# Attention scores with the queries' lower halves in zero-padded tiles of 128 rows

## The chip, the cores and the metric

The kernel runs on one core of one Trainium2 chip. The metric is device time in microseconds (us), the median over several runs. TensorE (PE in the rows) multiplies, and its weight loads have a row of their own (PEld). VectorE (DVE), ScalarE (ACT) and GpSimd (POOL) work element by element, and SyncE (SP) issues the transfers.

## The reference

Three transformer blocks on 512 tokens of width 1024: feed-forward layers around three kinds of mixer. Three attentions matter here. Each has eight sets of 64-wide queries and keys, and the third block, which has two of the three, runs twice. So there are five attentions in all.

```python
def forgetting_attention(q, k, v, log_f):            # first block
    ...
    for blk in range(s_ // Q_BLOCK):
        q0 = blk * Q_BLOCK
        q1 = q0 + Q_BLOCK
        logits = jnp.einsum('bhqd,bhkd->bhqk', q[:, :, q0:q1], k[:, :, :q1]).astype(jnp.float32) * scale
        ...
        p = jax.nn.softmax(logits, axis=-1).astype(v.dtype)
        outs.append(jnp.einsum('bhqk,bhkd->bhqd', p, v[:, :, :q1]))
...
def diff_mixer(q, k, v, lam, lam_init, g_subln):     # third block, "b"
        ...
        attn = p[:, 0] - lam * p[:, 1]
...
def dsa_mixer(q, k, v, iq, ik, iw):                  # third block, "a"
        ...
        _, idx = lax.top_k(score, topk)
        k_sel = gather(k, idx)
```

Queries stand in blocks of 128, and a block sees the keys up to its own end: 128, 256, 384 or 512 of them.

## The kernel before

The tokens are split in two halves of 256 (`hf` 0 and 1). Each phase (`f10`, `m1`, `f11`, ..., `m30`, `f30`, `m31`, `f31`) is written for half 0 and then for half 1, and priorities with a lag between the halves let a list scheduler weave them into one fixed order per engine when the program is built. While one half is in a mixer's attention, the other half's large products fill TensorE. The engines then run their orders strictly in sequence. `m1` is the first block's mixer, `m30` and `m31` are the third block's mixer in its two layers.

Numbers are held as two fp16 halves, upper and lower. For large products, `three` forms three matmuls of 128 rows by 256 columns: upper by upper, upper by lower, lower by upper. A head of the attention has only 64 rows, so the halves are stacked. `Heads` keeps a key's upper half on 64 rows and its lower half on the other 64 (tile `hd`). For queries the upper half stands twice in `hd`, and the lower half stands once, on the head's own 64 rows, in `hl`. In `scores`, one matmul over 128 rows then gives upper query times both halves of the key, and a second one over 64 rows adds lower query times upper key:

```python
mm(s[:, c0:c0 + n], q.t[j // 2][:, j % 2, e, c], k[:, :n], start=c0 == 0, stop=False)
mm(s[:, c0:c0 + n], q.low[r, j, c], k[r, :n], start=False, stop=False)
```

`e` is 0 or 1, and says which 64 rows are the head's. `keys(nk)` cuts the keys into pieces of at most 256, one for each half's tile. The 128 or 256 keys of a piece are the columns that the matmul streams. After the scores come a mask product, `softmax` (a maximum on VectorE, an exponential on ScalarE), `transposed` (TensorE, with a copy on ScalarE) and the product with the values.

In a printed form such as `64*128 64x256` the first number is the rows of the array that a matmul uses, and the last the columns streamed.

Query tiles come from the pool `mid` (`m2k`), which has 11 buffers for each half. The feed-forward layers' `act` tiles, the rotation tables, the indexer's scores and the attention's outputs come from the same pool. A buffer is given out again once its last tile has been read.

Of the kernel before, what the change touches and what calls it, by code (L numbers as in the profile page):

```python
# [11 lines left out]
F16 = mybir.dt.float16  # L12
# [7 lines left out]
TH = 256  # L20
# [36 lines left out]
# ---------------------------------------------------------------- host layout  # L57
# [99 lines left out]
def prepare(inp):  # L157
    a = {}
# [4 lines left out]
    # first block  # L163
# [21 lines left out]
    # second block  # L185
# [18 lines left out]
    # third block  # L204
# [36 lines left out]
# ---------------------------------------------------------------- the kernel  # L241

@with_exitstack
def tile_three_blocks(ctx: ExitStack, tc: tile.TileContext, d, col_at, con_at, out, phases=None):
# [42 lines left out]
    # ---- allocation  # L287
# [25 lines left out]
    def mm(out_, l, r, start=True, stop=True):  # L313
        return PE.matmul(out_, lhsT=l, rhs=r, start=start, stop=stop, skip_group_check=True)  # L314

    # ---- constants
# [33 lines left out]
    # ---- weights  # L350
# [45 lines left out]
    # ---- small functions  # L396
# [145 lines left out]
    # ---- conditioning of the first block  # L542
# [50 lines left out]
    # ---- token-major products  # L593
# [21 lines left out]
    # ---- softmax attention  # L615
# [20 lines left out]
    class Heads:  # L636
        """Eight heads of 64 rows, each as the fp16 halves of its values: stacked for keys, and for queries the
        upper half twice, with the lower half by itself."""

        def __init__(self, alloc, hf, query):  # L640
            self.t = [alloc(hf, [128, 2, 2, TH], F16, "hd") for _ in range(2)]
            self.low = alloc(hf, [128, 4, TH], F16, "hl") if query else None

        def put(self, j, src, scale=None):
            t = self.t[j // 2][:, j % 2]
            for e in range(2):
                a, b = slice(64 * e, 64 * e + 64), slice(64 - 64 * e, 128 - 64 * e)
                hi = t[a, e]
                lo = t[b, e] if self.low is None else self.low[a, j]
                if scale is None:  # L650
                    S.activation(hi, src[a], AF.Copy)
                    V.tensor_tensor(lo, src[a], hi, op=OP.subtract)
                else:
                    S.activation(hi, src[a], AF.Copy, scale=scale)
                    V.scalar_tensor_tensor(lo, src[a], scale, hi, op0=OP.mult, op1=OP.subtract)  # L655
                if self.low is not None:
                    S.activation(t[b, e], hi, AF.Copy)

    def scores(s, q, ks, j, e, c, nk):
        r = slice(64 * e, 64 * e + 64)  # L660
        for kh, c0, n in keys(nk):
            k = ks[kh].t[j // 2][:, j % 2, e]
            mm(s[:, c0:c0 + n], q.t[j // 2][:, j % 2, e, c], k[:, :n], start=c0 == 0, stop=False)
            mm(s[:, c0:c0 + n], q.low[r, j, c], k[r, :n], start=False, stop=False)
# [15 lines left out]
    # ---- the first block's mixer  # L680
# [3 lines left out]
    def mixer1(hf):  # L684
# [22 lines left out]
        # keys and queries  # L707
# [8 lines left out]
        # forget gates  # L716
# [26 lines left out]
        # values  # L743
# [5 lines left out]
        # attention  # L749
# [23 lines left out]
        # gated unit: projections  # L773
# [33 lines left out]
        # gated unit: spatial product  # L807
# [44 lines left out]
    # ---- the second block's mixer  # L852
# [3 lines left out]
    def mixer2(hf):  # L856
# [32 lines left out]
        # projections with token shift  # L889
# [23 lines left out]
        # convolution branch  # L913
# [32 lines left out]
        with boost(BOOST["m2k"]):  # L946
            wau = kv2k(0, name="wau")
            nc.sync.dma_start(out=wau, in_=d["m2_wa"])
            S.activation(xwa[0:64], xwa[0:64], AF.Tanh)
            S.activation(xg, xg, AF.Tanh, scale=0.5)  # L950
            V.tensor_scalar(xg, xg, 0.5, 0.5, op0=OP.mult, op1=OP.add)
            # key norms
            pn = psmall(hf, [8, TH], name="pkn")
            for q in range(4):
                t = t1k(hf, name="ksq")
                S.activation(t, kk_(q), AF.Square, scale=col("k_k", q))
                mm(pn, m2["sel8"][:, q * 8:q * 8 + 8], t, start=q == 0, stop=q == 3)
            kn = t1k(hf, [8, TH], name="kn")
            V.tensor_scalar(kn, pn, 1e-12, None, op0=OP.max)
            kr = t1k(hf, [8, TH], name="kr")  # L960
            rsqrt(hf, kn, kr)
            zb = {}
            wc = tin.tile([128, 4, 4], F32, name="wc", tag=f"wc{hf}", bufs=1)
            c64 = lambda ap: ap.rearrange("p (c t) -> p c t", c=2)

        def prep(pc):
            for q in range(4):
# [4 lines left out]
                # decay  # L972
# [12 lines left out]
                # write rate  # L985
# [4 lines left out]
                # normalised keys  # L990
# [20 lines left out]
        # values by token  # L1011
# [12 lines left out]
        # recurrence, by chunks  # L1024
# [63 lines left out]
        def chunk(c):  # L1088
# [5 lines left out]
            # products of queries and keys  # L1094
# [13 lines left out]
            # state in, corrections, outputs  # L1108
# [52 lines left out]
        with boost(BOOST["m2c"]):  # L1161
            mix = mixed[0]
            # gate
# [7 lines left out]
            # group norm and output  # L1171
# [49 lines left out]
    # ---- the third block's mixer  # L1221
# [3 lines left out]
    def mixer3(hf, l):  # L1225
# [37 lines left out]
        # projections of the indexer  # L1263
# [23 lines left out]
        # scores and selection  # L1287
# [41 lines left out]
        # projections and the difference of attentions  # L1329
# [15 lines left out]
        with boost(BOOST["m3b"]):  # L1345
            for qt in range(2):
                nk = (2 * hf + qt + 1) * 128
                nb = nk // 128
                # difference of attentions
# [21 lines left out]
        # projections of the selected attention  # L1371
# [15 lines left out]
        with boost(BOOST["m3a"]):  # L1387
            for qt in range(2):
                nk = (2 * hf + qt + 1) * 128
                nb = nk // 128  # L1390
                # selected attention
# [17 lines left out]
    # ---- the end  # L1409
# [10 lines left out]
    # ---- the order of the phases  # L1420
# [60 lines left out]
# ---------------------------------------------------------------- launch  # L1481
# [17 lines left out]
```

## Time and profile before

| | |
|---|---|
| median of 3 runs | 3520.48 us (3518.86 to 3536.04) |
| span of the profiled execution | 3506.1 us, from its first instruction to its last |
| PE busy | 3321.3 us (95%) |
| PEld busy | 2794.6 us (80%) |
| DVE busy | 2173.5 us (62%) |
| ACT busy | 1541.9 us (44%) |
| POOL busy | 0.2 us (four small memsets) |
| mean granted TensorE clock | 0.989 of full speed |

The profile gives the span alone of its execution; the median of the runs is 14.4 us above that span, which is what lies around it. Busy shares are means over stages that have different limits, so a stage is read for itself.

### The profile page before, as it was taken

To read this page: it belongs to the slowest core of one execution; us is meant where nothing else is said; L and a number is where in the kernel's file an instruction comes from. 1 tells how busy PE (TensorE), PEld (TensorE's weight loads), DVE (VectorE), ACT (ScalarE), POOL (GpSimd) and SP (SyncE) were. 2 spreads that over 40 slices of the span, in tenths; PEclk is the share of its full clock that TensorE was granted. 3 is DMA by queue.
4 is the path that set the end of the run, shared out by engine and by line. 5 is a ranking of instruction groups with operands and counts; after the bars stand their busy time and mean duration, and the time that the engine had idled before them with its cause. 6 is when DMAs were issued, how large, how long until landed. Compare 5 with 4: busy or idle time off the path is not lost.

```text
span 3506.1 us, 71906 instructions
## 1 busy us (share of the span) xinstructions
PE 3321.3 (95%) x30158; PEld 2794.6 (80%) x30164; DVE 2173.5 (62%) x5240; ACT 1541.9 (44%) x3335; POOL 0.2 (0%) x4
## 2 busy tenths in 40 slices
PE   5999999999999999997799998899999998999998
PEld 4888866788888888886578887667888876678887
DVE  8953757844374437588874438886544488855433
ACT  3332466433243324424243336886333378743331
POOL 0000000000000000000000000000000000000000
PEclk9999999999999999998899999999999999999999
DMA  8932313133223232201023232112232321023321
GB/s 275 324 112 91 118 55 130 61 103 103 97 92 103 98 102 91 76 5 35 31 74 106 100 105 79 55 49 67 91 103 104 100 78 61 31 79 109 102 98 48
DMA packets 105590, 327.88 MB, mean 94 GB/s; under 512 B 12584, under 2 KB 18088, under 8 KB 105008
## 3 DMA queue, kind: packets, MB, share of 16 engines
q1 hardware_dynamic: 105264, 323.28, 27.4%
q8 instruction: 236, 3.87, 0.4%
q14 instruction: 90, 0.74, 0.1%
HBM read 321.14 MB, written 2.10 MB: 92 GB/s over the span
## 4 chain that ended last, share of the span: by engine, by line
PE 75%; DVE 12%; ACT 9%; DMA 2%; issue 2%; SPq 0%; DVEq 0%; ACTq 0%
PE pgu L314 37%; PE po L314 19%; PE ps L314 5%; PE pp L314 4%; ACT rsw L1258 2%; PE pt L314 2%; DVE wr L363 2%; DVE mix L939 1%; ACT wr L362 1%; DMA st<-in_gu_dram 1%; PE pgl L314 1%; PE pxy L314 1%; DVE acc L433 1%; PE ps L631 1%; PE pT L314 1%
## 5 line engine op out<-in xcount | busy, mean ns | idle before, releaser
L314 PEld LDWEIGHTS <-wr 128*128 128x128 f16 x24000 | 2346.4, 98 | 322.7 <-issue 22.4
L314 PE MATMUL pgu<-hh,wr 128*128 128x256 f16 x12672 | 1400.1, 273 | 8.2 <-ACT wr L362 2.3
L363 DVE SCALAR_TENSOR_TENSOR wr<-st,wr 128x1024 f16<-128x1024 f32 x524 | 640.0, 1222 | 350.6 <-ACT wr L362 341.8
L314 PE MATMUL po<-act,wr 128*128 128x256 f16 x6336 | 700.3, 273 | 0.1
L362 ACT ACTIVATE wr<-st 128x1024 f16<-128x1024 f32 x524 | 551.5, 1053 | 322.5 <-PE pgu L314 127.6
L314 PE MATMUL pp<-hh,wr 128*128 128x256 f16 x3072 | 376.5, 273 | 4.0 <-DVE hd L655 1.2
L523 ACT ACTIVATE fth<-pgu 128x256 f32<-128x256 f32 x264 | 101.0, 383 | 587.2 <-PE pgu L314 587.1
L524 DVE SCALAR_TENSOR_TENSOR fth<-fth,pgu 128x256 f32<-128x256 f32 x264 | 110.8, 420 | 356.8 <-ACT fth L523 356.8
L314 PE MATMUL po<-mix,wr 128*128 128x256 f16 x1536 | 198.0, 281 | 15.8 <-ACT mix L444 9.0
L444 ACT ACTIVATE act<-fac 128x256 f16<-128x256 f32 x264 | 109.8, 416 | 179.1 <-DVE fac L526 179.1
L314 PE MATMUL pt<-wr,hh 128*128 128x512 f16 x576 | 146.2, 383 | 2.0 <-DVE wr L363 1.8
L445 DVE TENSOR_TENSOR act<-fac,act 128x256 f16<-128x256 f32 x264 | 111.2, 421 | 50.6 <-ACT act L444 50.2
L492 DVE TENSOR_TENSOR acc<-acc,sq 128x256 f32<-128x256 f32 x84 | 35.3, 420 | 149.6 <-ACT sq L491 149.6
L1258 ACT ACTIVATE rsw<-pp 32x256 f32<-32x256 f32 x304 | 114.1, 375 | 18.1 <-PE pp L314 13.6
L526 DVE SCALAR_TENSOR_TENSOR fac<-fth,pgu 128x256 f32<-128x256 f32 x264 | 110.7, 419 | 7.7
L619 DVE TENSOR_REDUCE amx<-ps 128x1 f32<-128x128 f32 (+3 forms) x160 | 77.8, 488 | 60.4 <-PE ps L314 55.7
L485 ACT ACTIVATE y<-po 128x256 f32<-128x256 f32 x64 | 24.4, 382 | 204.6 <-PE po L314 204.6
L432 ACT ACTIVATE sq<-x 128x256 f32<-128x256 f32 x154 | 56.3, 409 | 131.8 <-DVE x L501 127.4
L939 DVE SCALAR_TENSOR_TENSOR mix<-glu,cols,mix 128x256 f32<-128x256 f32 x240 | 101.9, 474 | 0.1
L314 PEld LDWEIGHTS <-hh 128*128 128x128 f16 x768 | 62.3, 100 | 48.0 <-issue 4.7
L565 DVE SCALAR_TENSOR_TENSOR ada<-adw,csil,ada 128x512 f32<-128x512 f32 x126 | 90.9, 744 | 7.2 <-DMA adw<-in_w_ada_dram 7.0
L501 DVE SCALAR_TENSOR_TENSOR x<-po,x 128x256 f32<-128x256 f32 x64 | 26.8, 421 | 106.8 <-PE po L314 106.8
(355 smaller groups left out, 2889.4 us busy)
## 6 DMA issues: line engine op xcount, KB each, us to landing
st<-in_gu_dram SPq DMA_DIRECT2D x264, 512.0 KB, 3.5
st<-in_dn_dram SPq DMA_DIRECT2D x132, 512.0 KB, 3.5
adw<-in_w_ada_dram SPq DMA_DIRECT2D x144, 256.0 KB, 5.5
st<-in_m_o_dram SPq DMA_DIRECT2D x32, 512.0 KB, 3.5
st<-in_m_b_dram SPq DMA_DIRECT2D x16, 512.0 KB, 3.5
st<-in_m_a_dram SPq DMA_DIRECT2D x16, 512.0 KB, 3.5
st<-in_m_s_dram SPq DMA_DIRECT2D x14, 512.0 KB, 3.5
st<-in_m_qk_dram SPq DMA_DIRECT2D x8, 512.0 KB, 4.4
```

The lines of the kernel that those rows point to most:

```text
L314: return PE.matmul(out_, lhsT=l, rhs=r, start=start, stop=stop, skip_group_check=True)
L362: S.activation(r[:, 0], st, AF.Copy, scale=WS)
L363: V.scalar_tensor_tensor(r[:, 1], st, WS, r[:, 0], op0=OP.mult, op1=OP.subtract)
L444: S.activation(hi, src, AF.Copy)
L445: V.tensor_tensor(lo, src, hi, op=OP.subtract)
L523: S.activation(t, p[:, 0], AF.Tanh, scale=0.5 / WS)
L524: V.scalar_tensor_tensor(t, t, 1.0, p[:, 0], op0=OP.add, op1=OP.mult)
L526: V.scalar_tensor_tensor(a, t, 0.5 / WS / WS / AS, p[:, 1], op0=OP.mult, op1=OP.mult)
L565: V.scalar_tensor_tensor(ada_acc[g, h], src, csil[:, k:k + 1], ada_acc[g, h], op0=OP.mult, op1=OP.add)
L619: V.tensor_reduce(nm, s[:, :nk], axis=AX.X, op=OP.max, negate=True)
L939: V.scalar_tensor_tensor(cc(j), gl[:, i:i + TH], dw[:, j * 31 + i:j * 31 + i + 1], cc(j), op0=OP.mult, op1=OP.add)
L1258: S.activation(sw[a:a + 32], p[c:c + 32], AF.Copy, scale=scale)
```

## The change

There are now two lower tiles per set of queries, one for each `e`. Each has 128 rows: the head's 64 rows carry the lower half, and the other 64 are set to zero on GpSimd when the tiles are made. The second score product then runs over all 128 rows, with the whole key tile as the moving side; the zero rows add nothing to the sum. The diff also replaces comments by blank lines, which moves line numbers by two to four.

```diff
         def __init__(self, alloc, hf, query):
             self.t = [alloc(hf, [128, 2, 2, TH], F16, "hd") for _ in range(2)]
-            self.low = alloc(hf, [128, 4, TH], F16, "hl") if query else None
+            self.low = [alloc(hf, [128, 4, TH], F16, "hl") for _ in range(2)] if query else None
+            if query:
+                for e in range(2):
+                    G.memset(self.low[e][64 - 64 * e:128 - 64 * e], 0.0)
...
-                lo = t[b, e] if self.low is None else self.low[a, j]
+                lo = t[b, e] if self.low is None else self.low[e][a, j]
...
     def scores(s, q, ks, j, e, c, nk):
-        r = slice(64 * e, 64 * e + 64)
         for kh, c0, n in keys(nk):
             k = ks[kh].t[j // 2][:, j % 2, e]
             mm(s[:, c0:c0 + n], q.t[j // 2][:, j % 2, e, c], k[:, :n], start=c0 == 0, stop=False)
-            mm(s[:, c0:c0 + n], q.low[r, j, c], k[r, :n], start=False, stop=False)
+            mm(s[:, c0:c0 + n], q.low[e][:, j, c], k[:, :n], start=False, stop=False)
```

The order of instructions on TensorE, VectorE and ScalarE is the same as before in all phases but `m30` and the stretch of `f30` that is woven with it. GpSimd has new work. Its order before, from the start of the program to its end:

```order
L1488 MEMSET const-float32-0.0 128x1
L1488 MEMSET const-float32-1.0 128x1
L1488 MEMSET const-bfloat16-1.0 128x1
L1488 MEMSET const-uint8-127 128x1
L1494 UNCONDITIONAL_BRANCH x2
```

And now, from the branch into the program on, with what each instruction waits for (semaphores of engines and of transfers; the first four `hl` are `m1`'s, the next two are `m30`'s half 0, "b", the next two half 0, "a", the last two shown half 1, "b"):

```order
L1496 UNCONDITIONAL_BRANCH [waits barrier_Pool_Activation_PE_DVE_SP_gather]
L645 MEMSET hl_4933 64x1024 [waits DVE_49,PE_49]
L645 MEMSET hl_4934 64x1024 [waits DVE_49,PE_49]
L645 MEMSET hl_6468 64x1024 [waits DVE_49,PE_49]
L645 MEMSET hl_6469 64x1024 [waits DVE_49,PE_49]
L645 MEMSET hl_26209 64x1024 [waits DVE_49,PE_49,Pool_49]
L645 MEMSET hl_26210 64x1024 [waits DVE_49,PE_49]
L645 MEMSET hl_26931 64x1024 [waits DMAHW2_49,DVE_49]
L645 MEMSET hl_26932 64x1024 [waits DMAHW1_49,DVE_49]
L645 MEMSET hl_28414 64x1024 [waits DMAHW7_49,PE_49,Activation_49]
L645 MEMSET hl_28415 64x1024 [waits PE_49,Activation_49,Pool_49]
```

Twenty memsets of 64 rows by 1024 elements are new, two for each of the ten sets of queries; each waits for the last users of the buffer that it takes.

The second place is TensorE in `m30`, where half 0's first score pass of "b" begins. Before (`pd` is the indexer's product, `ps` a score, `pp` a projection):

```order
L314 LDWEIGHTS iq
L314 MATMUL pd<-ik,iq 128x256
L314 LDWEIGHTS hd
L314 MATMUL ps<-hd 128x128
L314 LDWEIGHTS hl
L314 MATMUL ps<-hd,hl 128x128
L314 LDWEIGHTS identb
L314 MATMUL ps<-maskb,identb 128x128
L314 LDWEIGHTS wr
```

Now:

```order
L314 MATMUL pp<-hh,wr 128x256
L314 LDWEIGHTS iq
L314 MATMUL pd<-ik,iq 128x256
L314 LDWEIGHTS iq
L314 MATMUL pd<-ik,iq 128x256
L314 LDWEIGHTS hd
L314 MATMUL ps<-hd 128x128
L314 LDWEIGHTS hl
L314 MATMUL ps<-hd,hl 128x128
L314 LDWEIGHTS identb
L314 MATMUL ps<-maskb,identb 128x128
```

The same three products of a score stand together, but five projection matmuls have moved ahead of the two indexer products and the score. No order shows the rows of the array; the `hl` product has 64 before and 128 now.

The third place is VectorE in `m30`, where the two halves write their lower query tiles. Before (`hl_28402` is half 1's "b", `hl_26922` is half 0's "a"):

```order
L652 TENSOR_TENSOR hl_28402<-rot_28595,hd_28400 64x256
L1261 TENSOR_TENSOR rot_27095<-rot_27095,rsw_27126 128x256
L626 RECIPROCAL ars_26877<-asm_26875 128x1
L1311 MEMSET sc_28166 64x64
L363 SCALAR_TENSOR_TENSOR wr_27144<-st_27142,wr_27144 128x1024
L652 TENSOR_TENSOR hl_28402<-rot_28595,hd_28400 64x256
L1259 SCALAR_TENSOR_TENSOR rot_28635<-pp_28636,rope64_27993 128x256
L1260 TENSOR_TENSOR rsw_28661<-rsw_28661,rope64_27993 128x256
L652 TENSOR_TENSOR hl_26922<-rot_27095,hd_26920 64x256
```

Now (`hl_26932` is one of half 0's "a" tiles, `hl_28414` one of half 1's "b"):

```order
L405 TENSOR_SCALAR drs_26910<-drs_26910 128x4
L1261 SCALAR_TENSOR_TENSOR rot_28650<-pp_28651,rope64_28005 128x256
L1262 TENSOR_TENSOR rsw_28676<-rsw_28676,rope64_28005 128x256
L626 RECIPROCAL ars_27387<-asm_27385 128x1
L407 SCALAR_TENSOR_TENSOR rsa_26911<-drs_26910,dss_26780 128x4
L1263 TENSOR_TENSOR rot_28650<-rot_28650,rsw_28676 128x256
L408 TENSOR_TENSOR rsa_26911<-rsa_26911,drs_26910 128x4
L655 TENSOR_TENSOR hl_26932<-rot_27152,hd_26929 64x256
L409 SCALAR_TENSOR_TENSOR drs_26910<-rsa_26911,drs_26910 128x4
L1316 MAX m8_28250<-sc_28178 128x8
L407 SCALAR_TENSOR_TENSOR rsa_26911<-drs_26910,dss_26780 128x4
L655 TENSOR_TENSOR hl_28414<-rot_28570,hd_28412 64x256
```

Before, half 1's "b" query tiles came first and half 0's "a" after them; now half 0's "a" is written ahead of the first of half 1's "b".

## Rows read from the trace of the kernel before

**Rows 1.** The page: its span, and the busy time of TensorE and the others.

```profile
span 3506.1 us, 71906 instructions
PE 3321.3 (95%) x30158; PEld 2794.6 (80%) x30164; DVE 2173.5 (62%) x5240; ACT 1541.9 (44%) x3335; POOL 0.2 (0%) x4
```

**Rows 2.** Timeline, PE: start us, us, instruction, xcount, idle time before it.

```profile
3087.55 0.27 PE L314 MATMUL ps<-hd 128*128 128x256 f16 x1
3087.76 0.28 PE L314 MATMUL ps<-hd,hl 64*128 64x256 f16 x1
3087.97 0.28 PE L314 MATMUL ps<-hd 128*128 128x256 f16 x1
3088.18 0.28 PE L314 MATMUL ps<-hd,hl 64*128 64x256 f16 x1
3088.39 0.39 PE L314 MATMUL ps<-mb,identb 128*128 128x512 bf16 x1
...
460.29 0.22 PE L314 MATMUL ps<-hd 128*128 128x128 f16 x1
460.44 0.23 PE L314 MATMUL ps<-hd,hl 64*128 64x128 f16 x1
460.60 0.23 PE L314 MATMUL ps<-cum,sel 72*128 72x128 bf16 x1
```

**Rows 3.** Timeline, PE and PEld, where products without a 64-row one follow one another.

```profile
499.60 7.59 PE L314 MATMUL pp<-hh,wr 128*128 128x256 f16 x68
...
499.71 7.30 PEld L314 LDWEIGHTS <-wr 128*128 128x128 f16 x67
...
457.66 0.22 PE L314 MATMUL ps<-maskb,identb 128*128 128x128 bf16 x1
457.72 0.22 PE L314 MATMUL ps<-cum,sel 72*128 72x128 bf16 x1
```

**Rows 4.** Windows: us, busy of each engine, granted clock, DMA share, GB/s.

```profile
415.00:600.00 185.00, 179.74 (x1302) 123.06 (x1303) 128.01 (x375) 113.48 (x282) 0.00 (x0) 1.00 0.27 89
2150.00:2340.00 190.00, 167.33 (x1292) 117.54 (x1289) 168.96 (x492) 161.48 (x425) 0.00 (x0) 0.99 0.13 43
2340.00:2480.00 140.00, 138.13 (x1058) 104.05 (x1062) 92.04 (x238) 84.12 (x228) 0.00 (x0) 1.00 0.19 61
2840.00:3020.00 180.00, 157.13 (x1197) 108.86 (x1196) 157.19 (x461) 149.02 (x397) 0.00 (x0) 1.00 0.14 47
3020.00:3120.00 100.00, 98.57 (x716) 70.16 (x717) 66.23 (x167) 69.58 (x191) 0.00 (x0) 1.00 0.19 64
```

**Rows 5.** The same windows, instructions with `hl` alone: PE, PEld, DVE.

```profile
415.00:600.00 185.00, 12.57 (x48) 4.44 (x48) 6.73 (x16) 1.00 0.27 89
2150.00:2340.00 190.00, 11.34 (x44) 4.07 (x44) 9.95 (x24) 0.99 0.13 43
2340.00:2480.00 140.00, 13.79 (x52) 4.81 (x52) 3.32 (x8) 1.00 0.19 61
2840.00:3020.00 180.00, 12.81 (x50) 4.62 (x50) 9.97 (x24) 1.00 0.14 47
3020.00:3120.00 100.00, 12.33 (x46) 4.26 (x46) 3.31 (x8) 1.00 0.19 64
```

**Rows 6.** Chain that ended last, by line, shares of windows 2150:2340 and 2840:3020.

```profile
by line: ACT rsw L1258 19.6%; PE pp L314 10.4%; PE pt L314 8.6%; PE ps L314 8.0%; ACT hd L651 5.8%; issue 4.6%; ACT prob L624 4.6%; ACT wr L362 4.3%; ACT hd L657 3.9%; ACT rl L1305 2.5%; DVE hd L652 2.2%; ACT probt L633 2.2%; ACT ps L1364 1
...
by line: ACT rsw L1258 21.2%; PE ps L314 12.4%; PE pp L314 9.8%; PE pt L314 8.8%; ACT hd L651 8.2%; ACT prob L624 5.3%; ACT hd L657 4.8%; issue 4.2%; ACT wr L362 3.9%; ACT rl L1305 3.0%; ACT probt L633 2.5%; ACT hh L444 1.6%; ACT ps L1364 1
```

**Rows 7.** Those two windows, instructions with `ps` alone: PE, PEld, DVE, ACT.

```profile
2150.00:2340.00 190.00, 39.45 (x206) 10.71 (x88) 14.12 (x31) 32.20 (x114) 0.99 0.13 43
2840.00:3020.00 180.00, 45.65 (x245) 13.60 (x109) 15.07 (x35) 36.90 (x132) 1.00 0.14 47
```

**Rows 8.** Groups by line, memsets on VectorE and GpSimd: busy us, mean ns | idle.

```profile
L871 DVE MEMSET state<- 128x512 f32 x1 | 0.5, 485 | 0.1
...
L1488 POOL MEMSET const-uint8-127<- 128x1 uint8 x1 | 0.1, 102 | 0.0
```

## The prediction

> **What bounds the kernel now.** I read the page first: the span is 3506.1 us and TensorE is busy for 95% of it [rows 1]. With nothing else, that says only that TensorE matters. So the next view is the windows around the attentions [rows 4]. There the reader is to see two sorts of stretch. In 415 to 600 (`m1`), 2340 to 2480 (the end of `m30`) and 3020 to 3120 (the end of `m31`) TensorE is busy for 97 to 99%, and VectorE and ScalarE for 60 to 70%: what TensorE no longer does there is taken off the end. In 2150 to 2340 and 2840 to 3020 (the first parts of `m30` and `m31`) TensorE is at 87 to 88%, VectorE at 87 to 89%, ScalarE at 83 to 85%: three engines wait for one another in turn, and the chain there runs over ScalarE's rotation copies (20 and 21%) before any line of TensorE's [rows 6]. The same windows with `hl` alone count the second score products: 48, 44, 52, 50 and 46, 240 in all [rows 5].
>
> Then the timeline of single score products, where start to start counts and the printed lengths don't (they hold the latency of the array, which overlaps). Within a score of 512 keys the four products of 256 columns start at 3087.55, .76, .97 and 3088.18, and the mask product at 3088.39: 0.21 us each [rows 2]. Where every product uses all rows, 68 of the same 256 columns take 7.59 us, of which 0.27 is the last one's length: 7.32 / 67 = 0.109 us each, and their 67 weight loads lie beside them [rows 3]. So a product on 64 rows costs about 0.10 us more to go into and about 0.10 us more to leave. For 128 columns the steps are 0.15 and 0.16 us [rows 2], against 0.06 where two of 128 columns follow each other without a 64-row one [rows 3].
>
> **What the change removes.** A second product over 128 rows is the same kind of instruction as the first. Per product of 256 columns: from 0.84 us for two pairs to four times 0.109 = 0.436, so 0.40 / 2 = 0.20 us. Per product of 128 columns: 0.31 less two steps of 0.06, so 0.19 us. By the loops, each of five attentions with eight heads has per head two pieces of 128 columns (at 128 and 384 keys) and four of 256: 80 and 160 in all, which makes the 240 counted. Sum of TensorE's time: 160 x 0.20 + 80 x 0.19 = 47.2 us, 0.197 us on the mean.
>
> How much of it reaches the end is taken by stretch. In the three full ones lie 48 + 52 + 46 = 146 products: 146 x 0.197 = 28.8 us, taken whole. In the two mixed ones lie 94: 18.5 us, between nothing (ScalarE and VectorE set the pace, and TensorE only waits longer) and all of it. I choose by how much of the score work there lies on the chain: the line `ps` of the matmul helper has 8.0% of 190 us and 12.4% of 180 us, 15.2 + 22.3 = 37.5 us [rows 6], of 39.45 + 45.65 = 85.1 us of `ps` work on TensorE [rows 7]. That is 44%, so 8.1 us. Together 36.9 us.
>
> One rule speaks against this term. The rows show weight loads lying beside full-array products: 67 loads in 7.30 us under 68 matmuls in 7.59 [rows 3]. The Trainium skill (TensorE: Matmul & The Clock Gate, Part 3: Packing small matmuls) says that weight loads overlap with matmuls in flight only when they go to other row groups. By that rule a full second product would wait for its load behind the first, and padding would gain nothing; the rows of the full-array products don't bear it out, since there every load goes to all rows.
>
> **What it adds.** Twenty memsets of 64 x 1024 on GpSimd, which does nothing else. The trace has none of this size. VectorE's 128 x 512 memset takes 485 ns, GpSimd's 128 x 1 takes 102 ns [rows 8]. From below I take 0.1 us each, from above four times VectorE's rate, 4 x 2 x 0.485 = 3.9 us; it is nearest in kind to VectorE's, so 1 us, as an estimate. I put none of it on the path. The cover: a set's key projections stand ahead of its query projections, four of 24 matmuls, 96 x 0.109 = 10.5 us of TensorE, and the memset is issued where the set is made. Were that cover gone, the first score product of each tile would wait, 20 x 1 = 20 us, and the gain would be 17.
>
> VectorE writes as many elements to `hl` as before, in the same instructions. The weight load of an `hl` tile takes 92 ns on the mean (4.44 us for 48 [rows 5]), a full one at most 109 (67 in 7.30 us [rows 3]), and it lies beside the product before it. It costs nothing while products take 0.109; where products have 128 columns the load is the longer, and 0.06 to 0.07 a step is what the rows show.
>
> **What it moves.** One more buffer of `mid` is held for each set of queries. In `m1` and `m31` the orders are unchanged, so nothing moves. In `m30` half 0's first score falls behind five projection products on TensorE (0.5 us), and half 0's "a" tiles come ahead of half 1's "b" on VectorE; behind these stand the maxima and the selection, for which ScalarE's exponentials and then TensorE's transposes wait. Its price can't be read from an order. TensorE idles for 190 - 167.3 = 22.7 us in the first part of `m30` [rows 4]; a worse weave could add a third to it, a better one take a third away: -7 to +7 us. I take 0, since the same work stands in both orders and the end of `m30` is full of TensorE's work.
>
> **The sum.** 3506.1 - 36.9 = 3469.2 us of span. The profiled execution has no time of its own beside its span; the median of the runs is 14.4 us above it, and I carry that over: 3520.5 - 36.9 = 3483.6, 3484 us, 1.0% less.
>
> **The rivals.**
> All of it arrives: the mixed stretches are chains of products, softmax steps and copies, and a score that ends sooner lets its maximum start sooner. For it: in those windows TensorE waits in turn with the others, not for one alone. Against it: ScalarE's rotation copies lead the chain there. 3520.5 - 47.2 = 3473 us.
>
> Only the full stretches pay and `m30`'s new weave costs 7 us: 28.8 - 7 = 21.8, so 3499 us. Against it: half 0's scores move by half a microsecond only.
>
> The change doesn't do what it says: the second product waits for its own weight load even over full rows. Then a step costs 0.109 for the product and 0.09 to 0.11 for the load, 0.20 to 0.22 us, what it costs now, and the time stays at 3520 us. Against it stand the 67 loads beside full products.
>
> Slower: the zeros are late. In `m3` the memsets wait for buffers that VectorE, ScalarE and transfers must free, and they stand in one queue on GpSimd; TensorE stands in order, and the first weight load of each `hl` tile waits for GpSimd with all of the other half's products queued behind it. There are 16 such tiles in `m30` and `m31`. It makes the kernel slower than before from 36.9 / 16 = 2.3 us a tile on; with 5 us each, 80 - 36.9 = 43 us, 3564 us. Against it: the 10.5 us of key products ahead, and idle GpSimd.
>
> **How the numbers follow.** The forecast has 0.65, all of it 0.14, the full stretches alone with a bad weave 0.11, no effect 0.05, late zeros 0.05. The measurement can tell about 0.5%, 17.6 us, from no change, so faster means under 3503. Of the bad weave's 0.11 I count 0.07 as faster and 0.04 as the same (it may cost some more than 7). That gives faster 0.86, same 0.09, slower 0.05. The likeliest time is 3484; the range reaches from 3468 (all of it, with 5 us from a better weave) to 3503 (the full stretches alone, less 11 us for weave and memsets), which leaves out no effect, late zeros and a part of the bad weave.
>
> **What would show it.** In the profile after: score products in a row start 0.11 us apart with 256 columns and 0.06 to 0.07 with 128; the printed shape is `128*128` for all 480. `m1` from its first to its last score is shorter by about 48 x 0.197 = 9.5 us. The first parts of `m30` and `m31` are shorter by 3 to 5 us each, and TensorE's busy share there falls. GpSimd's memsets end before VectorE writes the same tile's query halves, and no weight load of `hl` waits for GpSimd. The prediction is wrong if the steps stay at 0.2 us, if `m30` gets longer while `m31` gets shorter (weave), or if waits of TensorE for `hl` and GpSimd appear.

## The result, and the profile after

The changed kernel takes 3507.4 us (median of 5 runs, 3493.8 to 3521.6), the kernel before 3523.4 us (5 runs beside them). The ratio is 0.9939 with an interval of 0.991 to 0.9968: about 0.6% faster. In two later sets of runs the ratio was 0.9967 (0.995 to 0.9985) and 0.9933 (0.9908 to 0.9958). So the gain is 0.3 to 0.7%, 12 to 24 us, where 36.9 us and 1.0% were forecast. 3507 lies 4 us above the range's upper end; by the ratio and the 3520.5 us from which the sum was made it is 3499.

The page of the changed kernel, its span and busy times, against [rows 1]:

```profile
span 3506.0 us, 71986 instructions
PE 3309.1 (94%) x30164; PEld 2815.7 (80%) x30164; DVE 2171.3 (62%) x5240; ACT 1545.5 (44%) x3335; POOL 19.1 (1%) x24
```

By these two pages nothing was won: 3506.0 us now, 3506.1 before. They are single executions, and the reader should not stop here; where they differ is shown below.

The timeline of TensorE in the changed kernel, at the score of 512 keys that [rows 2] shows:

```profile
3087.66 0.27 PE L314 MATMUL ps<-hd 128*128 128x256 f16 x1
3087.77 0.27 PE L314 MATMUL ps<-hd,hl 128*128 128x256 f16 x1
3087.88 0.27 PE L314 MATMUL ps<-hd 128*128 128x256 f16 x1
3087.99 0.27 PE L314 MATMUL ps<-hd,hl 128*128 128x256 f16 x1
3088.10 0.38 PE L314 MATMUL ps<-mb,identb 128*128 128x512 bf16 x1
```

The steps are 0.11 us where they were 0.21, and the shape is `128*128`. Four products take 0.44 us in place of 0.84. With 128 columns the steps are 0.06 us, as the rows of 2958.49 and 2958.55 below show.

The windows of the changed kernel. Their edges lie at the same instructions as those of [rows 4], so the lengths can be compared; only the edges at 2350.5 and 2488.5, where the order has moved, are the nearest that fit (columns: window; us; busy of PE, PEld, DVE, ACT, POOL; granted clock; DMA share; GB/s):

```profile
414.50:593.50 179.00, 173.17 (x1303) 123.78 (x1304) 127.69 (x375) 113.69 (x282) 0.00 (x0) 1.00 0.28 91
2160.50:2350.50 190.00, 164.01 (x1289) 120.85 (x1286) 168.44 (x496) 158.33 (x421) 4.73 (x5) 0.96 0.13 43
2350.50:2488.50 138.00, 131.53 (x1063) 104.46 (x1061) 92.22 (x235) 88.65 (x233) 0.00 (x0) 1.00 0.19 62
2848.40:3024.40 176.00, 149.85 (x1197) 110.54 (x1195) 156.26 (x461) 149.27 (x397) 1.89 (x2) 0.99 0.16 49
3024.40:3119.10 94.70, 91.77 (x717) 70.69 (x717) 65.64 (x168) 69.48 (x191) 0.00 (x0) 1.00 0.22 68
```

Against [rows 4] the five windows are shorter by 6.0, 0.0, 2.0, 4.0 and 5.3 us. That is 17.3 us of 36.9. The two windows of `m30` give 2.0, where 3.8 + 10.2 = 14.0 were forecast (44 x 0.197 x 44%, and 52 x 0.197). The granted clock of the first of them is 0.96, where it was 0.99; more on that below.

GpSimd's memsets, as a group of the changed kernel (busy us, mean ns | idle before them, by releaser):

```profile
L645 POOL MEMSET hl<- 64x1024 f16 x20 | 18.9, 946 | 2938.2 <-PE po L314 2249.0 <-DVE acc L492 371.8 <-DVE rsw L1262 109.6
```

One takes 0.946 us; 1 us was the estimate. In each of the three profiles of the changed kernel a single wait of TensorE or its weight loads is put down to GpSimd, in `m31`, and it is 1.0 us long. The rows around it, in this profile:

```profile
2956.59 0.94 POOL L645 MEMSET hl<- 64x1024 f16 x1 [74.97 <-DVE rsa L407]
...
2958.28 0.27 PE L314 MATMUL ps<-hd 128*128 128x256 f16 x1 [0.72 <-ACT rl L1307]
2958.28 0.10 PEld L314 LDWEIGHTS <-hl 128*128 128x128 f16 x1 [1.00 <-POOL hl L645]
...
2958.49 0.22 PE L314 MATMUL ps<-hd 128*128 128x128 f16 x1
...
2958.55 0.22 PE L314 MATMUL ps<-hd,hl 128*128 128x128 f16 x1
```

The memset had ended at 2957.54, 0.74 us before the load began. The load began together with the product ahead of it, and that one had waited for ScalarE's `rl`. So the memset isn't what held TensorE there.

**Why two equal spans hide a gain.** The rows of a tile give the starts of its first and of its last instruction, and so the ends of a phase. Three lengths were taken, all from start to start: `m1` from its first to its last score product (`ps<-hd`), from the first rotation copy (`rsw<-pp`) of `m30` to that of `m31` (`m30` with `f30`), and from there to the last score product of `m31`. The rows of the kernel before, by tile (count: shortest/median/longest ns, first to last start; shapes):

```profile
L314 PE MATMUL ps<-hd x48: 216/269/283, 431.2 to 575.5; 128*128 128x256 f16 x32, 128*128 128x128 f16 x16
...
L1258 ACT ACTIVATE rsw<-pp x152: 373/375/380, 2143.4 to 2364.6; 32x256 f32<-32x256 f32 x152
...
L1258 ACT ACTIVATE rsw<-pp x152: 373/375/378, 2800.0 to 3043.8; 32x256 f32<-32x256 f32 x152
...
L314 PE MATMUL ps<-hd x96: 216/269/283, 2850.5 to 3101.8; 128*128 128x256 f16 x64, 128*128 128x128 f16 x32
```

Of the changed kernel:

```profile
L314 PE MATMUL ps<-hd x48: 216/269/283, 430.7 to 568.8; 128*128 128x256 f16 x32, 128*128 128x128 f16 x16
...
L1260 ACT ACTIVATE rsw<-pp x152: 373/376/378, 2153.8 to 2376.5; 32x256 f32<-32x256 f32 x152
...
L1260 ACT ACTIVATE rsw<-pp x152: 373/376/382, 2808.4 to 3047.0; 32x256 f32<-32x256 f32 x152
...
L314 PE MATMUL ps<-hd x96: 216/269/417, 2858.9 to 3101.0; 128*128 128x256 f16 x64, 128*128 128x128 f16 x32
```

`m1` took 575.5 - 431.2 = 144.3 and takes 138.1 us; `m30` with `f30` took 656.6 and takes 654.6; `m31` took 301.8 and takes 292.6. The three together are 17.4 us shorter. But from `m1`'s last score product to `m30` it took 1567.9 us before and takes 1585.0, 17.1 more, and no score product lies there. The windows of 1340 to 1800 us, in the second block's mixer `m2`, show what differs; first the kernel before in its first profile, then the changed kernel, then the kernel before profiled again:

```profile
1340.00:1800.00 460.00, 405.90 (x4830) 334.99 (x4828) 380.58 (x1144) 191.31 (x440) 0.00 (x0) 0.93 0.15 50
```

```profile
1340.00:1800.00 460.00, 406.33 (x4690) 333.99 (x4688) 366.66 (x1097) 184.94 (x425) 0.00 (x0) 0.89 0.15 47
```

```profile
1340.00:1800.00 460.00, 410.11 (x4660) 336.17 (x4657) 362.15 (x1088) 182.19 (x418) 0.00 (x0) 0.87 0.15 46
```

The granted clock is 0.93, 0.89 and 0.87, and the same 460 us hold 4830, 4690 and 4660 matmuls. The kernel before thus has both the quick and the slow version of this stretch: profiled again, it reaches `m30` 2163.3 - 2143.4 = 19.9 us later, while its three lengths are 144.3, 656.6 and 301.7 us, the same to 0.1. What `m2` does to a span differs from execution to execution and is as large as the effect looked for; the three lengths of the kernel before are not touched by it. They are the measure in what follows, beside the timed ratios. They aren't free of the clock either: the changed kernel's `m30` with `f30` took 654.6, 653.1 and 651.9 us in three executions of the same order, with 13.7, 10.2 and 6.8 us of it at the lower clock level, 1.2 GHz.

### The profile page after: what moved, and what is told of

Its sections match the earlier page's. It is cut to its first block, busy times and chain, and to the rows that moved or that the text cites. A ratio compares the mean times of both kernels' runs of the same rounds, so it can differ in the third digit from the quotient of the medians.

```text
span 3506.0 us, 71986 instructions
## 1 busy us (share of the span) xinstructions
PE 3309.1 (94%) x30164; PEld 2815.7 (80%) x30164; DVE 2171.3 (62%) x5240; ACT 1545.5 (44%) x3335; POOL 19.1 (1%) x24
## 5 line engine op out<-in xcount | busy, mean ns | idle before, releaser
L314 PEld LDWEIGHTS <-wr 128*128 128x128 f16 x24000 | 2351.0, 99 | 327.8 <-issue 25.5
L314 PE MATMUL pgu<-hh,wr 128*128 128x256 f16 x12672 | 1402.6, 273 | 7.9 <-ACT wr L362 2.3
L314 PE MATMUL po<-act,wr 128*128 128x256 f16 x6336 | 702.0, 273 | 0.1
L314 PE MATMUL pp<-hh,wr 128*128 128x256 f16 x3072 | 384.1, 274 | 4.8 <-DVE rot L1261 2.2
L314 PE MATMUL po<-mix,wr 128*128 128x256 f16 x1536 | 198.0, 282 | 15.9 <-ACT mix L444 9.0
L314 PE MATMUL pt<-wr,hh 128*128 128x512 f16 x576 | 145.4, 383 | 1.6 <-DVE wr L363 1.6
L314 PEld LDWEIGHTS <-hh 128*128 128x128 f16 x768 | 62.2, 100 | 48.3 <-issue 3.2
```

## The experiments

Twelve runs were made, of seven further kernels and of the two that are compared. What was timed (median of all runs in us; ratio to the kernel before on the same chip, with its interval) and the three lengths, as differences from 144.3, 656.6 and 301.8 us:

| kernel | timed | ratio | `m1` | `m30` + `f30` | `m31` | together |
|---|---|---|---|---|---|---|
| changed kernel | 3507.4 | 0.9939 (0.991 to 0.9968) | -6.2 | -2.0 | -9.2 | -17.4 |
| e0_after | 3512.9 | 0.9967 (0.995 to 0.9985) | -6.5 | -4.7 | -9.5 | -20.7 |
| a_again | 3499.7 | 0.9933 (0.9908 to 0.9958) | -5.0 | -3.5 | -10.1 | -18.6 |
| e1_full_one_tile | 3494.5 | 0.9916 (0.9893 to 0.9939) | -6.5 | -7.9 | -9.7 | -24.1 |
| e1_again | 3493.4 | 0.9919 (0.9892 to 0.9945) | -6.5 | -8.3 | -9.6 | -24.4 |
| e2_two_tiles_64 | 3524.7 | 1.0006 (0.9987 to 1.0026) | 0.0 | +4.9 | -0.2 | +4.7 |
| e2_again | 3513.2, one run | | 0.0 | +4.8 | +0.5 | +5.3 |
| h2_no_memset_64 | 3521.3, one run | | 0.0 | -1.2 | +1.2 | 0.0 |
| e3_grouped | 3508.0 | 0.9958 (0.9937 to 0.9979) | -3.1 | -4.5 | -3.8 | -11.4 |
| f1_pool_copy | 3489.8 | 0.9904 (0.9878 to 0.993) | -7.1 | -8.5 | -14.9 | -30.5 |
| b_again (the kernel before) | 3528.0, one run | | 0.0 | 0.0 | -0.1 | -0.1 |
| d0_double_copy | 3533.7, one run | | +1.5 | +5.7 | +14.2 | +21.4 |
| d1_double_copy_full | 3522.2, one run | | -5.2 | +0.7 | +6.5 | +2.0 |

The theory was that a change between 64-row and 128-row products costs time on either side of a 64-row one, and that a part of what is shed is lost to `m30`'s new weave and to waits in the full stretches. The rivals were that the second tile and the zeros cost the difference directly, and that the 64-row product itself is slow.

**The full second product without second tiles** (e1_full_one_tile). The kernel before, with one line changed. The one lower tile holds the other head's lower half on the other 64 rows, so each score gets one term more, that half by this key's lower half.

```diff
-            mm(s[:, c0:c0 + n], q.low[r, j, c], k[r, :n], start=False, stop=False)
+            mm(s[:, c0:c0 + n], q.low[:, j, c], k[:, :n], start=False, stop=False)
```

> The kernel before with one edit: the second score product runs over all 128 rows of the single lower tile and of the key tile. No zeros, no memset, no second tile. The rows of the other head are not zero, so the scores also get the other head's lower query half times this key's lower half, which the kernel before leaves out. My theory (the steps of the products fall from 0.2 to 0.11 us, about 0.12 us of each 0.197 reaches the end in full stretches, and the extra tiles' new weave in m30 costs some us): about 25 to 32 us faster than before, 3 to 8 us better than the changed kernel. Rival one, the new weave costs nothing: the same as the changed kernel within 3 us. Rival two, the second product is slow for its zero rows or its two tiles: no faster than the changed kernel, whatever the order.

Ratio 0.9916, 27.6 us by the medians, where 25 to 32 were expected. Against the changed kernel it is better by 18.4 us in this set of runs (e0_after) and by 6.4 in the next, where 3 to 8 were expected; the repeats below bear on that. In `m1` and `m31` it gains what the changed kernel does, in `m30` 7.9 us in place of 2.0 to 4.7. Its rotation rows give that length, 2798.3 - 2149.6 = 648.7 us:

```profile
L1258 ACT ACTIVATE rsw<-pp x152: 372/374/380, 2149.6 to 2366.9; 32x256 f32<-32x256 f32 x152
...
L1258 ACT ACTIVATE rsw<-pp x152: 372/374/378, 2798.3 to 3036.4; 32x256 f32<-32x256 f32 x152
```

So the product over all rows is the gain, and what comes with the two tiles takes some of it back in `m30`. This kernel's order isn't wholly that of before: VectorE and ScalarE keep it in `m1` and in `m30` up to 2366 us of the first trace, and some fifty instructions of each are moved behind that, most of them at the end of `m30`.

**The two tiles without the full product** (e2_two_tiles_64). The tiles, the memsets and the order of the changed kernel, with the second product on 64 rows:

```diff
-            mm(s[:, c0:c0 + n], q.low[e][:, j, c], k[:, :n], start=False, stop=False)
+            r = slice(64 * e, 64 * e + 64)
+            mm(s[:, c0:c0 + n], q.low[e][r, j, c], k[r, :n], start=False, stop=False)
```

> The changed kernel with the second score product put back to 64 rows: the two lower tiles, the twenty memsets and the new order in m30 stay. My theory: 0 to 7 us slower than before, all of it in m30; m1 and m31 as before within 1 us. Rival (tiles, memsets and weave are free): the same as before within 2 us in every mixer. Second rival (late zeros): waits of TensorE's weight loads of the lower tiles for GpSimd, 2 us or more each.

Ratio 1.0006. `m1` and `m31` stay within 0.2 us; `m30` becomes 4.9 us longer:

```profile
L1261 ACT ACTIVATE rsw<-pp x152: 372/374/377, 2154.1 to 2379.7; 32x256 f32<-32x256 f32 x152
...
L1261 ACT ACTIVATE rsw<-pp x152: 372/374/378, 2815.6 to 3059.3; 32x256 f32<-32x256 f32 x152
```

661.5 us against 656.6. The padding's companions cost about 5 us, all in the one phase whose order moved; 0 to 7 were expected. The effects add up: -24.1 + 4.7 = -19.4, and the changed kernel has -17.4 to -20.7.

**The 64-row products side by side** (e3_grouped). The kernel before, with a score's upper products first and its 64-row ones behind them:

```diff
-        for kh, c0, n in keys(nk):
-            k = ks[kh].t[j // 2][:, j % 2, e]
-            mm(... q.t[j // 2][:, j % 2, e, c], k[:, :n], start=c0 == 0, stop=False)
-            mm(... q.low[r, j, c], k[r, :n], start=False, stop=False)
+        for low in range(2):
+            for kh, c0, n in keys(nk):
+                k = ks[kh].t[j // 2][:, j % 2, e]
+                if low:
+                    mm(... q.low[r, j, c], k[r, :n], start=False, stop=False)
+                else:
+                    mm(... q.t[j // 2][:, j % 2, e, c], k[:, :n], start=c0 == 0, stop=False)
```

> The kernel before, with the products of a score in another order: with two key pieces, both upper products first and then both 64-row ones. Theory one (the cost is the change between 128 and 64 rows, paid once going in and once coming out): two 64-row products in a row start 0.11 us apart or less, a pair of changes goes away in each of the 80 scores with two pieces, 80 x 0.2 = 16 us of TensorE, of which 60% reach the end: 10 us faster than before, half of what the change gives. Rival (a 64-row product itself takes 0.2 us): steps stay at 0.2 us throughout and the time stays within 2 us of before.

Ratio 0.9958. The timeline of TensorE at a score of 384 keys, where each row holds two products, of 256 and of 128 columns:

```profile
2411.18 0.33 PE L314 MATMUL ps<-hd 128*128 128x256 f16 x2
2411.44 0.34 PE L314 MATMUL ps<-hd,hl 64*128 64x256 f16 x2
2411.71 0.34 PE L314 MATMUL ps<-mb,identb 128*128 128x384 bf16 x1
```

Two full products without a change would take 0.109 + 0.06 = 0.17 us [rows 3]. Each pair here takes 0.26 to 0.27, so there is one change of 0.10 us per pair, and none between the two 64-row products. The 64-row product is not slow; changing to it from 128 rows and back is, at 0.10 us each way. The Trainium skill (TensorEngine Tiling (Array Packing), Key Properties) says that changing the tiling mode drains TensorE, and gives no time; these rows fit that and give one, though no row shows the drain itself. Not every change of rows has this price: the mask product of `m1` over 72 rows starts 0.06 us after one over 128 [rows 3], but 0.16 us after one over 64 [rows 2]. Grouping takes away a third of the 240 alternations, 80 x 0.197 = 15.8 us of TensorE; 11.4 arrived by the lengths and 14.2 by the medians, where 10 were expected.

**Repeats of the changed kernel and of e1** (e0_after, a_again, e1_again), and the kernel before profiled beside them (b_again).

> The changed kernel once more, on the same chip as the other three. Theory one (the 14 us that the profiled run loses in the second block's mixer come from a lower granted clock there that differs from execution to execution): this execution's clock in that mixer differs from the one seen, and its time with it; the ratio to before lies at 0.991 to 0.997 again. Rival (the change lowers the clock there): the same 95 us at the lower of the two clock levels in the mixer, against 61 us before, in this execution too.

> The changed kernel a third time. If its lower mean clock (0.979 in most of its executions so far, 0.984 for the kernel before) comes from the kernel, it is 0.978 to 0.982 again here, its ratio is 0.995 to 0.997, and it lies about 15 us above the kernel with one tile. If it is chance, its clock is that of the kernel before within 0.002, and its ratio is 0.994, 7 us or less above the kernel with one tile.

> The kernel before, unedited, for one more profile. Theory one (the half-speed stretches of TensorE's clock in the second block's mixer differ from execution to execution): this profile has another sum of them between 1340 and 1800 us than the 61 us of the first one, by 10 us or more, and a span that is longer by up to half of that. Rival (the kernel before always has 61 us there, and only the changed kernel more): 61 us within 4 us again.

> The kernel with one lower tile and full products again, beside the changed kernel: 0.9916 of before again within 0.002, a clock of 0.983 to 0.987, if what it saves against the changed kernel is not chance. If it is, it lies within 4 us of the changed kernel.

The changed kernel's profiles had a mean granted clock of 0.980, 0.978 and 0.984, e1's 0.984 twice, and the kernel before had 0.989 and then 0.980. In e0_after all 11 executions lay at 0.977 to 0.982, beside 0.978 to 0.989 for the kernel before; in a_again the ten lay at 0.980 to 0.987. So a mean clock as low as e0_after's does not come with the changed kernel each time. Why it held there in all 11 is not shown. The ratios of e1 agree to 0.0003, those of the changed kernel spread by 0.0034.

**What the weave's 5 us is** (h2_no_memset_64, with e2_again beside it). Two tiles and 64-row products as in e2, and no memset; the 64 other rows are never read.

```diff
-            if query:
-                for e in range(2):
-                    G.memset(self.low[e][64 - 64 * e:128 - 64 * e], 0.0)
```

> Two lower tiles and 64-row products as in the kernel with the products put back, but without the twenty memsets. It separates the second tile's buffer from the memset that claims it early; what counts is the time from the first rotation of the third block's first mixer to the first of its second (656.6 us before, 661.5 with tiles and memsets). Theory one (the memsets claim the buffers before the query halves come, and the order suffers): 655 to 658 us. Rival (the second buffer alone is the cost): 660 to 663 us.

> Two lower tiles, memsets and 64-row products again. If the 4.9 us in the third block's first mixer belong to the order, 660 to 663 us from first rotation to first rotation; if they are chance, 655 to 658.

The rotation rows of h2:

```profile
L1258 ACT ACTIVATE rsw<-pp x152: 373/375/379, 2155.8 to 2376.7; 32x256 f32<-32x256 f32 x152
...
L1258 ACT ACTIVATE rsw<-pp x152: 373/375/378, 2811.2 to 3024.4; 32x256 f32<-32x256 f32 x152
```

`m30` with `f30` takes 655.4 us, 1.2 less than before, and in e2_again 4.8 more. The second buffer of `mid` by itself is therefore not the cost; the 5 us come with the memsets. They also change the scheduler's order, since they stand in its list with waits of their own: on VectorE and ScalarE h2 keeps the order of before up to 2365 us of the first trace, and e2 only up to 2181.

The traces of e2 speak for the order and against the memsets' own waits. In neither does TensorE, VectorE or ScalarE wait for GpSimd. But TensorE's indexer products (`pd`) wait longer for ScalarE's `rl`, which in the new order stands behind other copies. First the kernel before, then e2, in the 345 us from the first rotation of `m30` (us in total, times, longest):

```profile
PE pd L314 <- ACT rl L1305: 1.5, 2, 0.9
```

```profile
PE pd L314 <- ACT rl L1308: 5.7, 4, 2.5
```

Two of these waits, 2.9 us in all, lie in the 12 us that begin 130 us behind that rotation. Before, and in e2 (columns as above):

```profile
2273.40:2285.40 12.00, 11.26 (x61) 5.29 (x60) 11.11 (x39) 10.59 (x28) 0.00 (x0) 1.00 0.00 1
```

```profile
2284.10:2296.10 12.00, 9.08 (x47) 4.76 (x45) 9.87 (x25) 10.84 (x25) 0.64 (x1) 0.86 0.01 1
```

The granted clock falls there to 0.86, in all five executions with tiles and memsets; in both of the kernel before, both of e1 and in h2 it is 1.00. Other waits of TensorE for ScalarE are shorter in e2 (10.4 us for its exponentials and copies in the attentions, against 13.5), so how the 5 us divide between waits and clock stays open. A kernel with the changed order and no memset was not tried.

**Do ScalarE's steps swallow the rest?** (d0_double_copy, d1_double_copy_full.) The copy of the transposed probabilities on ScalarE is made twice, in the kernel before and in e1:

```diff
         S.activation(ps[:, :nk], pt[:, :nk], AF.Copy)
+        S.activation(ps[:, :nk], pt[:, :nk], AF.Copy)
```

> The kernel before with ScalarE's copy of the transposed probabilities done twice (the second writes the same values), so each head's chain of score, softmax, transpose, copy and value product is about 0.43 us longer on ScalarE. Its partner is the next kernel; what counts is their difference. Alone: TensorE's weight loads wait longer for this copy than the 6.7 us of the kernel before in its first attention, and that attention takes longer.

> The same doubled copy in the kernel with one lower tile and full products. Without it the full products save 9.5 us of TensorE in the first attention, of which 6.3 arrive. Theory one (the missing third is TensorE waiting for ScalarE's softmax steps, which come no sooner): with a longer chain less arrives, 2 to 5 us of the 9.5 in the first attention, and 6 to 8 us instead of 9.7 in the last mixer. Rival (the third goes into weight loads and steps that have lost their cover, whatever ScalarE does): 6.3 and 9.7 us again, within 0.7.

One run each, 3533.7 and 3522.2 us. d0's `m1` is 1.5 us longer than before, as expected, but its weight loads wait 3.4 us for the second copy, not more than 6.7. d1 is shorter than d0 by 6.7 us in `m1`, 5.0 in `m30` with `f30` and 7.7 in `m31`, 19.4 in all. With single copies the same step gave 24.1. `m1` does not gain less than with single copies (6.5), as the rival has it, while the 7.7 of `m31` lie where theory one has them. Waits of weight loads for ScalarE's exponentials and copies grow in `m1` from 6.7 to 11.1 us between the two. The second copy also made the scheduler weave anew from `m1` on, so this pair differs from the pair with single copies in more than the copy, and the test is inconclusive.

**A version that goes further** (f1_pool_copy). e1, with the second copy of a query's upper half moved from ScalarE to idle GpSimd:

```diff
-                    S.activation(t[b, e], hi, AF.Copy)
+                    G.tensor_copy(t[b, e], hi)
```

> The kernel with one lower tile and full products, and the second copy of each query's upper half moved from ScalarE to GpSimd: 80 copies of 414 ns, 33 us less for ScalarE, most of it in the first parts of the third block's mixers where ScalarE leads the chain. Theory one (ScalarE's queue sets the pace there): 3 to 8 us faster than the kernel with one tile. Rival (GpSimd takes 1 us or more for such a copy and the scores wait for it, or VectorE, as busy as ScalarE, sets the pace): within 2 us of it, or slower.

Ratio 0.9904, the lowest of all; its interval overlaps e1's, but `m31` is 5.2 us shorter than e1's. The copies as a group on GpSimd:

```profile
L657 POOL COPY hd<-hd 64x256 f16<-64x256 f16 x80 | 45.9, 574 | 3001.7 <-ACT hd L651 2501.2 <-DVE x L476 432.0 <-ACT hd L654 66.7
```

The copies take GpSimd 0.574 us on the mean, 0.40 to 1.47 each, and relieve ScalarE, the engine whose rotation copies lead the chain in the mixed stretches [rows 6]. That this relief is the cause is not shown: hundreds of instructions of ScalarE and VectorE also stand elsewhere than in e1, from `m1` on, and TensorE and its weight loads wait 6.3 us for GpSimd's copies.

## Why the prediction was right, and where its sizes were off

**The mechanism and its price: right.** The steps fell to 0.11 and 0.06 us as forecast, and e3 shows in another way that the 0.10 us belong to the change between 128 and 64 rows. By these steps TensorE sheds 240 products' worth, 47.2 us. What was off is how much of that reaches the end: about half of the 36.9 us.

**"28.8 us, taken whole": the first term mis-sized.** In the two full stretches whose order did not move, 6.0 to 6.2 of 9.5 us arrived (`m1`) and 5.3 of 9.1 (end of `m31`): about 0.6, not all. (Over the three profiles `m1` gave 5.0 to 6.5.) The waits of TensorE's weight loads show where the rest stands. First `m1` before (415 to 600), then now (414.5 to 593.5): us in total, times, longest.

```profile
PEld L314 <- issue: 11.8, 40, 1.3
PEld ps L314 <- ACT probt L633: 6.7, 19, 0.8
...
PEld ps L631 <- ACT prob L624: 1.0, 4, 0.4
```

```profile
PEld ps L314 <- ACT probt L633: 9.0, 27, 0.7
PEld L314 <- issue: 6.6, 22, 1.3
...
PEld ps L631 <- ACT prob L624: 2.5, 9, 0.5
```

Then the end of `m31` before (3020 to 3120), and now (3024.4 to 3119.1):

```profile
PEld L314 <- issue: 7.9, 31, 0.5
PEld ps L314 <- ACT probt L633: 6.7, 21, 0.6
...
PEld ps L631 <- ACT prob L624: 0.7, 2, 0.4
```

```profile
PEld ps L314 <- ACT probt L633: 9.5, 25, 0.8
PEld ps L631 <- ACT prob L624: 1.9, 6, 0.5
PEld L314 <- issue: 1.5, 4, 0.6
```

Waits with no releaser ("issue") shrink by 5.2 and 6.4 us, and waits for ScalarE's exponentials and copies grow by (9.0 + 2.5) - (6.7 + 1.0) = 3.8 and (9.5 + 1.9) - (6.7 + 0.7) = 4.0. If the first kind is counted with the changes of rows, the sums nearly close: 6.0 + 3.8 = 9.8 of 9.5, and 5.3 + 4.0 = 9.3 of 9.1. The prediction took a busy share of 97 to 99% for a stretch in which nothing else is waited for. It isn't one: the printed length of a matmul holds 0.16 us more than its step (0.27 against 0.11), and so hides about half of a wait of 0.3 us. The transposes and value products already stood behind ScalarE by 7.7 us in `m1`; scores that end sooner only reach that wait sooner. That is an account from rows; the test of its cause (d0, d1) did not confirm it.

**"I take 0" for the weave in `m30`: wrong inside its own bounds.** It was bounded at -7 to +7 us; e2 measured +4.9 and +4.8, and the changed kernel's `m30` is 3.2 to 6.3 us longer than e1's, the clock of the executions included. The argument, that the same work stands in both orders, doesn't hold: e1 has the same work too, in an order nearer to that of before, and gains 7.9 us there. What the new order added was waits of TensorE for ScalarE's `rl` and a stretch at a lower clock.

**44% of the mixed stretches: met in `m31`, missed in `m30`.** The first part of `m31` gave 4.0 of 50 x 0.197 = 9.85 us, 41%. In the changed kernel's `m30` the weave covers it, but e1 keeps the order of before through the first part of `m30`. The same two copies on ScalarE, before and in e1:

```profile
2150.86 0.18 ACT L1286 ACTIVATE iw<-piw 128x16 f32<-128x16 f32 x1
...
2339.19 0.60 ACT L1382 ACTIVATE va<-pt 128x512 f32<-128x512 f32 x1
```

```profile
2157.02 0.18 ACT L1286 ACTIVATE iw<-piw 128x16 f32<-128x16 f32 x1
...
2343.52 0.60 ACT L1382 ACTIVATE va<-pt 128x512 f32<-128x512 f32 x1
```

188.33 us became 186.50: 1.8 of 44 x 0.197 = 8.7 us, 21% (2.5 in e1_again). The 44% was also worked out from unlike terms: the chain's line is that of L314 alone, while the 85.1 us of `ps` hold the transposes of L631 too, 67 of 0.27 us, some 18 us. So the hit in `m31` is in part luck. The whole of `m30` in e1 gave 7.9 of 18.9 us, where the working had 14.0.

**The memsets: right.** They took 0.946 us each, and no memset held TensorE: the one wait that the profile puts down to GpSimd is not the memset's, as shown above. What they cost came by way of the order of `m30`, which has a term of its own above.

**The base: misread, without harm to the forecast.** The 14.4 us between span and median are not "what lies around" the span: the changed kernel's profiled execution took 3507.87 us for a span of 3506.0, 1.9 us around it. The first profile was of a quick execution of `m2`, and b_again took 3528.03 us for a span of 3526.0. The sum came out as median less gain all the same, which is the right base.

**Together:** 36.9 us were forecast, and 17.4 to 20.7 arrived by the three lengths. The weave took some 5, and the full stretches gave 0.6 of what they shed. 3499, the time by the ratio, lies in the range because its upper end allowed for a dear weave and dear memsets; full stretches that pay in part were not allowed for.

**The rivals.** All of it arrives (3473): no, about half does even without the second tiles (e1, 24.1 of 47.2). The second product waits for its own load: no, the steps are 0.11 us with a load each. The rule of the Trainium skill (TensorE: Matmul & The Clock Gate, Part 3: Packing small matmuls), that weight loads overlap only when they go to other row groups, doesn't describe these loads over all rows. Late zeros: no. The full stretches alone with a weave of 7 us (3499) came nearest in time, for a partly different reason: the mixed part of `m31` paid, and the full stretches paid 0.6.

## What to carry to other kernels

Where products over 64 rows stand between products over 128, count the alternations and price both directions from start-to-start steps; padding with zeros removes them, grouping like with like removes a part without any new tile, and leaving the neighbour's small term in the rows, where the result can bear it, needs no zeros at all. A stretch in which TensorE is busy for 98% is not yet bound by TensorE alone: look at the waits of its weight loads, since short waits hide under the printed lengths. And compare phases by the same two instructions in both traces, with the granted clock of the phase beside them, before believing two spans, since a stretch with a varying clock can hide or feign a gain of half a per cent.

## What the runs showed of the hardware that was not expected

A change between 128 and 64 rows costs 0.10 us each way, and the next product of the same kind costs nothing extra (two 64-row products of 256 and 128 columns and the change behind them: 0.27 us). A 72-row product behind one of 128 rows pays nothing (0.06 us, [rows 3]). GpSimd's memset of 64 x 1024 fp16 took 0.946 us, its copy of 64 x 256 fp16 0.574 us on the mean. And the granted clock of one stretch of an unchanged kernel was 0.93 in one execution and 0.87 in another, worth 19.9 us by the start of the next mixer, about as much as the whole effect measured here.
